# MLP up-projection as seven block products instead of the plain product

## The chip, the cores and the metric

One core of a Trainium2 chip runs the kernel. The metric is device time in microseconds (us), lower is better. The kernel before took 2957.06 us, the median of 2 runs (2955.55 to 2958.57). The engines are TensorE (PE, matrix products), VectorE (DVE), ScalarE (ACT), GpSimd (POOL) and SyncE (SP, which issues the DMA transfers).

## The reference

One layer of a bidirectional encoder over 512 tokens of width 2048: neighbourhood attention and a gated delta scan are projected, gated and mixed, and an MLP follows. Only the MLP and what stands just ahead of it matter here:

```python
    mixed = jax.nn.sigmoid(gate_a) * (y_a @ w_proj_a) + jax.nn.sigmoid(gate_b) * (y_b @ w_proj_b)
    h = h + mixed @ w_out                                    # 2048 x 2048
    hn = _rmsnorm(h, norm_mlp_w)
    h = h + jnp.square(jax.nn.relu(hn @ w_mlp_up)) @ w_mlp_down   # 2048 x 8192, 8192 x 2048
return _rmsnorm(h, norm_final_w)
```

All of it is float32.

## The kernel before

A float32 product is made from three fast products. Every operand is split into a high part (a rounded copy, made by an ACT cast) and a low part (source minus high part, made by a DVE subtract), and each 128x128 weight block takes part in three matmuls: high by high, high by low, low by high (`unit_mm`, lines 106 to 119; the matmuls are L115, L116 and L117). Weights come from HBM in units of 128x1024 (512 KB, `load_raw`, DMA on SP at L82) into one of 4 buffers; `load_unit` splits a unit by an ACT cast (L89) and a DVE subtract (L90) into one of 3 buffer pairs `wh`, `wl`. A unit serves eight 128x128 blocks, 24 matmuls with all 512 tokens as the moving tile. The activations stay in SBUF as pairs of 128x512 tiles, transposed (channels on the partitions), most of them in the pool `big` of 48 tiles.

The stages of interest follow one another:

- w_out (L850 to L864, tiles `ps_b<-mh,wh_wo`): 16 output tiles m, two units each. L855 adds x, L856 stores the sum, L861/L862 scale it by the norm weight and split it into `hh`, `hl`, and `sumsq` (L821 to L827) gathers squares. For m of 8 and more, `hh` and `hl` lie in a separate pool `hq` on the right side of SBUF, else in `big`.
- `stat` turns the sums of squares into the factor `rB` per token (matmuls L833/L834, a chain of small DVE operations L142 to L145, matmul L149, ACT copy). It runs beside the first matmuls of the next stage.
- MLP up (L866 to L879, tiles `ps_b<-hh,wh_up`): 64 output tiles m, two units each. L872 takes relu and multiplies by `rB`, L873 squares, L874 stores the 128x512 result to HBM (`hidD`). From m = 41 on, every second m one finished hidden tile is loaded back and split (`load_hid`, L841 to L844), 11 in all, so that the next stage finds them.
- MLP down (L887 to L896): four passes over 16 hidden tiles each, accumulated in `Ha`, which is first loaded from HBM (L881/L882).
- The last two output tiles of the last pass use half the tokens at a time: 128x256 matmuls, L926 to L928. The final norm ends the kernel.

A scheduler in the framework fixes the order of each engine's instructions when the kernel is built; all DMA issues of these stages share SP's one queue. An engine executes in that order and waits on semaphores. A buffer that is reused is written only after its last reader is done; a pool that is opened after another one was closed takes over its space under the same rule.

## Time and profile before

| what | value |
|---|---|
| median of the runs | 2957.06 us (2955.55 to 2958.57) |
| span of the profiled execution | 2960.0 us |
| PE busy | 98% of the span |
| DVE busy | 46% |
| ACT busy | 29% |
| DMA | 411.95 MB, mean 139 GB/s |
| w_out stage | 1360.1 to 1534.2 us |
| MLP up stage | 1534.2 to 2243.9 us |
| MLP down stage | 2243.9 to 2918.8 us, halves to 2943.2 us |

The page sums each engine's busy time over the whole span. A matmul's own duration in it overlaps those of its neighbours, so the rate of PE is read from the number of matmuls in a stretch or from the distance of their starts. Where an engine's idle time ends, the page names what was waited for last.

### The profile page before, as it was taken

The numbers are of one execution on the slowest core, as the hardware profiler recorded it, in microseconds if no ns is written. First come the engines' busy times: TensorE is split into PE (matmuls) and PEld (weight loads), VectorE is DVE, ScalarE is ACT, GpSimd is POOL, SyncE is SP. The second block draws the span as 40 slices with busy tenths as digits, with TensorE's granted clock in tenths as the row PEclk, the third lists the DMA queues.
The fourth block names the chain that finished last, engine by engine and source line by source line (L and its number), as shares of the span: only waits on it lengthen the run. The fifth ranks groups of instructions, "written<-read, shape, count | busy, mean of one in ns | idle before, by whom it ended". The sixth has DMA issues, their size and how long they took to land.

```text
span 2960.0 us, 33906 instructions
## 1 busy us (share of the span) xinstructions
PE 2913.1 (98%) x13432; PEld 2397.5 (81%) x13432; DVE 1365.7 (46%) x2071; ACT 872.6 (29%) x1333; POOL 24.7 (1%) x66
## 2 busy tenths in 40 slices
PE   8999999999999999999999999999999999999998
PEld 6778788888788888888888888888888888888887
DVE  6888769744554443444342222223333242332333
ACT  6444322233233333222222222222223131221322
POOL 0000000000000000000000000000000000000000
PEclk9999999999999999999999999999999999999999
DMA  7556653655532223443433333334336243342322
GB/s 228 185 182 186 207 185 118 219 153 171 183 114 96 91 85 132 160 155 117 148 125 114 123 119 118 120 118 136 128 129 230 94 155 100 107 143 94 113 100 86
DMA packets 170847, 411.95 MB, mean 139 GB/s; under 512 B 34368, under 2 KB 46720, under 8 KB 170688
## 3 DMA queue, kind: packets, MB, share of 16 engines
q1 hardware_dynamic: 170016, 407.69, 41.7%
q0 software_dynamic: 672, 2.10, 0.3%
q8 instruction: 105, 1.72, 0.2%
q14 instruction: 54, 0.44, 0.0%
HBM read 350.84 MB, written 58.88 MB: 138 GB/s over the span
## 4 chain that ended last, share of the span: by engine, by line
PE 72%; DVE 0%; SPq 0%; DMA 0%; ACT 0%; issue 0%; DVEq 0%; POOL 0%
PE ps_b L115 20%; PE ps_b L116 20%; PE ps_b L117 20%; PE ps_mm L117 4%; PE ps_mm L115 3%; PE ps_mm L116 3%; PE ps_ax L676 0%; PE ps_b L926 0%; PE ps_b L927 0%; PE ps_b L928 0%; DVE Ha L906 0%; PE ps_ax L137 0%; PE ps_ax L690 0%; PE ps_ax L692 0%; PE ps_ax L691 0%; PE ps_ax L657 0%
## 5 line engine op out<-in xcount | busy, mean ns | idle before, releaser
L115 PE MATMUL ps_mm<-xh,wh_in 128*128 128x512 f32 x1416 | 567.3, 401 | 3.4 <-ACT wh_in L89 3.4
L117 PE MATMUL ps_mm<-xh,wl_in 128*128 128x512 f32 x1416 | 560.6, 396 | 1.3 <-DVE wl_in L90 1.3
L116 PE MATMUL ps_mm<-xl,wh_in 128*128 128x512 f32 x1416 | 560.0, 395 | 0.0
L115 PE MATMUL ps_b<-hh,wh_up 128*128 128x512 f32 x1024 | 402.0, 393 | 0.0
L117 PE MATMUL ps_b<-hh,wl_up 128*128 128x512 f32 x1024 | 401.7, 392 | 0.0
L116 PE MATMUL ps_b<-hl,wh_up 128*128 128x512 f32 x1024 | 401.5, 392 | 0.0
L116 PE MATMUL ps_b<-hil,wh_dn 128*128 128x512 f32 x992 | 385.8, 389 | 0.0
L117 PE MATMUL ps_b<-hih,wl_dn 128*128 128x512 f32 x992 | 385.7, 389 | 0.0
L115 PE MATMUL ps_b<-hih,wh_dn 128*128 128x512 f32 x992 | 385.7, 389 | 0.0
L117 PEld LDWEIGHTS ps_mm<-xh,wl_in 128*128 128x128 f32 x1416 | 267.8, 189 | 62.3 <-DVE wl_in L90 2.6
L115 PEld LDWEIGHTS ps_mm<-xh,wh_in 128*128 128x128 f32 x1416 | 267.7, 189 | 59.1 <-ACT wh_in L89 4.0
L116 PEld LDWEIGHTS ps_mm<-xl,wh_in 128*128 128x128 f32 x1416 | 267.8, 189 | 54.7 <-issue 0.2
L89 ACT CAST wh_in<-raw_in 128x1024 fp32r<-128x1024 f32 x177 | 186.0, 1051 | 414.5 <-PE ps_mm L116 325.7
L89 ACT CAST wh_up<-raw_up 128x1024 fp32r<-128x1024 f32 x128 | 134.6, 1052 | 529.1 <-PE ps_b L116 300.0
L90 DVE TENSOR_TENSOR wl_up<-raw_up,wh_up 128x1024 fp32r<-128x1024 f32 x128 | 156.8, 1225 | 274.5 <-ACT wh_up L89 274.5
L90 DVE TENSOR_TENSOR wl_in<-raw_in,wh_in 128x1024 fp32r<-128x1024 f32 x177 | 216.2, 1222 | 121.4 <-ACT wh_in L89 114.8
L89 ACT CAST wh_dn<-raw_dn 128x1024 fp32r<-128x1024 f32 x124 | 130.9, 1055 | 477.1 <-PE ps_b L116 461.5
L90 DVE TENSOR_TENSOR wl_dn<-raw_dn,wh_dn 128x1024 fp32r<-128x1024 f32 x124 | 151.9, 1225 | 244.4 <-ACT wh_dn L89 244.1
L116 PEld LDWEIGHTS ps_b<-hl,wh_up 128*128 128x128 f32 x1024 | 192.2, 188 | 43.8 <-issue 0.2
L115 PEld LDWEIGHTS ps_b<-hh,wh_up 128*128 128x128 f32 x1024 | 192.2, 188 | 43.6 <-issue 0.2
L117 PEld LDWEIGHTS ps_b<-hh,wl_up 128*128 128x128 f32 x1024 | 192.1, 188 | 43.4
L116 PEld LDWEIGHTS ps_b<-hil,wh_dn 128*128 128x128 f32 x992 | 186.2, 188 | 38.9 <-DVE hil L95 0.2
(307 smaller groups left out, 3203.1 us busy)
## 6 DMA issues: line engine op xcount, KB each, us to landing
raw_in<-in_win SPq DMA_DIRECT2D x177, 512.0 KB
raw_up<-in_wup SPq DMA_DIRECT2D x128, 512.0 KB
raw_dn<-in_wdn SPq DMA_DIRECT2D x124, 512.0 KB
raw_wo<-in_wout SPq DMA_DIRECT2D x32, 512.0 KB
hidD<-ur SPq DMA_DIRECT2D x64, 256.0 KB
hr<-hidD SPq DMA_DIRECT2D x64, 256.0 KB
gD<-g SPq DMA_DIRECT2D x32, 256.0 KB
raw_pa<-in_wpa SPq DMA_DIRECT2D x16, 512.0 KB
```

The lines of the kernel that those rows point to most:

```text
L89: S_.copy(out=hi, in_=raw)
L90: V.tensor_tensor(out=lo, in0=raw, in1=hi.bitcast(F32), op=ALU.subtract)
L115: PE.matmul(ps, hi[:, w], rh, start=first and kk == 0, stop=False)
L116: PE.matmul(ps, hi[:, w], rl, start=False, stop=False)
L117: PE.matmul(ps, lo[:, w], rh, start=False, stop=last and kk == 7)
```

## The change

The up-projection is rewritten as a block product of the Strassen family (Winograd's form, with seven products). Rows and columns of the weight are halved: for an iteration i the four 128x1024 weight units A11, A12 (output tile m0 = i//8*16 + i%8, its two halves of the contraction) and A21, A22 (output tile m0 + 8) face the four quarters of the activations, X11, X21 (contraction halves, first 256 tokens) and X22 (second contraction half, last 256 tokens) with X12 only inside combinations. There are 32 iterations. Each makes four sums of weight units on DVE (128x1024): S1 = A21 + A22, S3 = A21 + A11, S2 = S1 + A11, S4 = S2 + A12 (signs are absorbed elsewhere), and seven products of 24 matmuls with 128x256 moving tiles: A11 by X11, S2 by T2, S1 by T1, A12 by X21, S3 by T3, S4 by X22, A22 by T4. T1 to T4 are combinations of the quarters, made once. Seven weight operands per iteration are split by ACT and DVE where the kernel before split four units for the same two output tiles. The epilogue combines the products in 128x256 pieces: two ACT copies out of PSUM and nine DVE operations, then two squares and two stores of 128x512.

What moves with it: the w_out loop visits its tiles in the order 0, 8, 1, 9 and so on; the scaling (now L868) comes after the squares; each pair of tiles makes X11 (in a new right-side pool `bq`), X21, X22 and four 128x256 combinations into a tile `TR` of a right-side pool `tr`; after the last pair 32 splits turn these into T2, T1, T3, T4. Then `tr` is closed and the pool `sm` (raw buffers for A21, the sums, small temporaries) is opened on the same space. The first iteration takes its S4 product second. The 11 early loads of hidden tiles are gone; 16 `load_hid` follow the loop.

In the order of DVE, around the start of the changed stage (XT*o*_*j* are the 128x256 low halves of T*o*; S1_0 is the sum S1 of iteration 0, `wl_` a low half of a weight operand), the change has:

```order
L95 TENSOR_TENSOR XT4_5_12137<-TR5_11742,XT4_5_12137 128x256
L95 TENSOR_TENSOR XT4_6_12140<-TR6_11894,XT4_6_12140 128x256
L95 TENSOR_TENSOR XT4_7_12143<-TR7_12045,XT4_7_12143 128x256
L926 TENSOR_TENSOR S1_0_12158<-raw_A21_0_12152,raw_A22_0_12154 128x1024
L927 TENSOR_TENSOR S3_0_12159<-raw_A21_0_12152,raw_A11_0_12150 128x1024
L934 TENSOR_TENSOR S2_0_12170<-S1_0_12158,raw_A11_0_12150 128x1024
L936 TENSOR_TENSOR S4_0_12171<-S2_0_12170,raw_A12_0_12156 128x1024
L95 TENSOR_TENSOR wl_S4_0_12231<-S4_0_12171,wh_S4_0_12230 128x1024
L95 TENSOR_TENSOR wl_A12_0_12262<-raw_A12_0_12156,wh_A12_0_12261 128x1024
```

All 32 splits of the combinations stand ahead of the first weight sum on DVE, and that sum reads raw_A21_0. On SP at the same place (raw_A11_0 is the load of A11 of iteration 0):

```order
L82 DMA raw_A11_0_12150<-in_wup 128x1024 [waits DMAHW7_49,DVE_49]
L82 DMA raw_A22_0_12154<-in_wup 128x1024 [waits DMAHW0_49,DVE_49]
L866 DMA hTD_93<-xr14_11820 128x512 [waits DMAHW1_49,DVE_49]
L82 DMA raw_A12_0_12156<-in_wup 128x1024 [waits DMAHW2_49,DVE_49]
L82 DMA raw_A11_1_12415<-in_wup 128x1024 [waits DMAHW5_49,DMAHW3_49,DVE_49]
L866 DMA hTD_93<-xr7_11900 128x512 [waits DMAHW4_49,DVE_49]
L866 DMA hTD_93<-xr15_11972 128x512 [waits DVE_49]
L893 DMA raw_A21_0_12152<-in_wup 128x1024 [waits DMAHW6_49,DVE_49]
L893 DMA raw_A21_1_12417<-in_wup 128x1024 [waits DMAHW7_49]
```

The load of A21_0 waits for a DVE instruction, the last of the 32 splits (XT4_7), whose source shares the space of its buffer; the other three units of iteration 0 are loaded ahead of it. In the middle of the stage DVE had in the kernel before, for one output tile, two low halves and one epilogue operation:

```order
L90 TENSOR_TENSOR wl_up40_0_14616<-raw_up40_0_14613,wh_up40_0_14615 128x1024
L90 TENSOR_TENSOR wl_up40_1_14646<-raw_up40_1_14643,wh_up40_1_14645 128x1024
L872 SCALAR_TENSOR_TENSOR ur39_14608<-ps_b_14547,rB_79 128x512
L90 TENSOR_TENSOR wl_up41_0_14681<-raw_up41_0_14678,wh_up41_0_14680 128x1024
L90 TENSOR_TENSOR wl_up41_1_14711<-raw_up41_1_14708,wh_up41_1_14710 128x1024
```

and now for a cycle of two output tiles (i = 4, with sums for i = 5; from the low half of A11 of i = 4 on):

```order
L95 TENSOR_TENSOR wl_A11_4_13143<-raw_A11_4_13120,wh_A11_4_13142 128x1024
L956 TENSOR_TENSOR u2_3_12902<-ps_b_12899,u2_3_12902 128x256
L957 SCALAR_TENSOR_TENSOR ur3_12903<-u2_3_12902,rB_79 128x256
L95 TENSOR_TENSOR wl_S2_4_13173<-S2_4_13140,wh_S2_4_13172 128x1024
L961 TENSOR_TENSOR t1_3_12900<-ps_b_12898,t1_3_12900 128x256
L926 TENSOR_TENSOR S1_5_13363<-raw_A21_5_13357,raw_A22_5_13359 128x1024
L962 SCALAR_TENSOR_TENSOR ur11_12904<-t1_3_12900,rB_79 128x256
L95 TENSOR_TENSOR wl_S1_4_13202<-S1_4_13128,wh_S1_4_13201 128x1024
L927 TENSOR_TENSOR S3_5_13364<-raw_A21_5_13357,raw_A11_5_13355 128x1024
L95 TENSOR_TENSOR wl_A12_4_13231<-raw_A12_4_13126,wh_A12_4_13230 128x1024
L941 TENSOR_TENSOR u2_4_13137<-ps_b_13133,t1_4_13135 128x256
L95 TENSOR_TENSOR wl_S3_4_13260<-S3_4_13129,wh_S3_4_13259 128x1024
```

Between two low halves there stands a sum or an epilogue operation of 128x256 now. The load of A22 of the following iteration reuses the buffer that the low half of A11 frees.

The diff:

```diff
--- before.py
+++ after.py
@@ -843,10 +843,20 @@
             nc.sync.dma_start(out=raw, in_=hidD[k])
             return split(raw, big(f"hih{k}"), big(f"hil{k}"))
 
-        hT = []
+        p7 = ExitStack()
+        bq = p7.enter_context(tc.tile_pool(name="bq", bufs=8, side="right", reuse_waits="tile"))
+
+        def operand(src, name):
+            t = bq.tile([128, T], F32R, tag="B2", name=name) if name.startswith("X11") else big(name)
+            return split(src, t[:, 0:256], t[:, 256:512])
+
+        lo_t, hi_t = slice(0, 256), slice(256, 512)
+        XS = {}
         with ExitStack() as p5:
-            hq = p5.enter_context(tc.tile_pool(name="hq", bufs=1, side="right", reuse_waits="tile"))
-            for m in range(16):
+            tr = p5.enter_context(tc.tile_pool(name="tr", bufs=8, side="right", reuse_waits="tile"))
+            TR = []
+            xs = []
+            for n, m in enumerate(m for j in range(8) for m in (j, j + 8)):
                 ps = bank()
                 xr = ev(f"xr{m}")
                 nc.sync.dma_start(out=xr, in_=xT[:, m, :])
@@ -854,26 +864,106 @@
                     unit_mm(ps, load_unit(wout[m, u], f"wo{m}_{u}"), mix, 8 * u, u == 0, u == 1)
                 V.tensor_tensor(out=xr, in0=ps, in1=xr, op=ALU.add)
                 nc.sync.dma_start(out=hTD[m], in_=xr)
-                if m < 8:
-                    hh, hl = big(f"hh{m}"), big(f"hl{m}")
+                sq = sumsq(xr, n, f"h{m}")
+                S_.activation(out=xr, in_=xr, func=AF.Copy, scale=nlw_s[:, m : m + 1])
+                xs.append(xr)
+                if n % 2 == 0:
+                    XS["11", m] = operand(xr[:, lo_t], f"X11_{m}")
                 else:
-                    hh, hl = hq.tile([128, T], F32R, name=f"hh{m}"), hq.tile([128, T], F32R, name=f"hl{m}")
-                S_.activation(out=hh, in_=xr, func=AF.Copy, scale=nlw_s[:, m : m + 1])
-                V.scalar_tensor_tensor(out=hl, in0=xr, scalar=nlw_s[:, m : m + 1], in1=hh.bitcast(F32), op0=ALU.mult, op1=ALU.subtract)
-                hT.append((hh, hl))
-                sq = sumsq(xr, m, f"h{m}")
+                    j = n // 2
+                    x0, x1 = xs[n - 1], xs[n]
+                    XS["21", j] = operand(x1[:, lo_t], f"X21_{j}")
+                    XS["22", j] = operand(x1[:, hi_t], f"X22_{j}")
+                    t = tr.tile([128, 4, 256], F32, tag="tr", name=f"TR{j}")
+                    V.tensor_tensor(out=t[:, 0], in0=x0[:, lo_t], in1=x0[:, hi_t], op=ALU.subtract)
+                    V.scalar_tensor_tensor(out=t[:, 1], in0=t[:, 0], scalar=-1.0, in1=x1[:, hi_t], op0=ALU.mult, op1=ALU.subtract)
+                    V.tensor_tensor(out=t[:, 2], in0=x1[:, hi_t], in1=x0[:, hi_t], op=ALU.subtract)
+                    V.scalar_tensor_tensor(out=t[:, 3], in0=t[:, 1], scalar=-1.0, in1=x1[:, lo_t], op0=ALU.mult, op1=ALU.subtract)
+                    TR.append(t)
             tasks.append(stat("h", sq))
-            hid0 = []
-            for m in range(64):
-                ps = bank()
-                for u in range(2):
-                    unit_mm(ps, load_unit(wup[m, u], f"up{m}_{u}"), hT, 8 * u, u == 0, u == 1)
-                r = ev(f"ur{m}")
-                V.scalar_tensor_tensor(out=r, in0=ps, scalar=0.0, in1=rB, op0=ALU.max, op1=ALU.mult)
-                S_.activation(out=r, in_=r, func=AF.Square)
-                nc.sync.dma_start(out=hidD[m], in_=r)
-                if m >= 40 and m % 2 == 1 and len(hid0) < 11:
-                    hid0.append(load_hid(len(hid0)))
+            for o, e in (("T2", 1), ("T1", 0), ("T3", 2), ("T4", 3)):
+                for j in range(8):
+                    XS[o, j] = operand(TR[j][:, e], f"X{o}_{j}")
+
+        with ExitStack() as p6:
+            sm = p6.enter_context(tc.tile_pool(name="sm", bufs=1, side="right", reuse_waits="tile"))
+
+            def load_a(src, name):
+                raw = sm.tile([128, 1024], F32, tag="a", name=f"raw_{name}", bufs=2)
+                nc.sync.dma_start(out=raw, in_=src)
+                return raw
+
+            def sums(name, bufs=4):
+                return sm.tile([128, 1024], F32, tag="sum", name=name, bufs=bufs)
+
+            def et(name):
+                return sm.tile([128, 256], F32, tag="et", name=name, bufs=6)
+
+            def wsplit(raw, name):
+                hi = st.tile([128, 1024], F32R, tag="wh", name=f"wh_{name}", bufs=3)
+                lo = st.tile([128, 1024], F32R, tag="wl", name=f"wl_{name}", bufs=3)
+                return split(raw, hi, lo)
+
+            def product(ps, w, o, first=False):
+                hi, lo = w
+                for j in range(8):
+                    rh, rl = XS[o, j]
+                    c = slice(j * 128, (j + 1) * 128)
+                    PE.matmul(ps, hi[:, c], rh, start=first and j == 0, stop=False, skip_group_check=True)
+                    PE.matmul(ps, hi[:, c], rl, start=False, stop=False, skip_group_check=True)
+                    PE.matmul(ps, lo[:, c], rh, start=False, stop=j == 7, skip_group_check=True)
+                    if j % NPUMP == NPUMP - 1:
+                        pump()
+
+            for i in range(32):
+                m0 = i // 8 * 16 + i % 8
+                m1 = m0 + 8
+                a11 = load_raw(wup[m0, 0], f"A11_{i}")
+                a21 = load_a(wup[m1, 0], f"A21_{i}")
+                a22 = load_raw(wup[m1, 1], f"A22_{i}")
+                a12 = load_raw(wup[m0, 1], f"A12_{i}")
+                s1, s3 = sums(f"S1_{i}"), sums(f"S3_{i}")
+                V.tensor_tensor(out=s1, in0=a21, in1=a22, op=ALU.add)
+                V.tensor_tensor(out=s3, in0=a21, in1=a11, op=ALU.add)
+                a, b, c = (bank()[:, 0:256] for _ in range(3))
+                t1, t5, u2 = et(f"t1_{i}"), et(f"t5_{i}"), et(f"u2_{i}")
+                r0, r1 = ev(f"ur{m0}"), ev(f"ur{m1}")
+                s2, s4 = sums(f"S2_{i}"), sums(f"S4_{i}")
+                product(a, wsplit(a11, f"A11_{i}"), "11", True)
+                S_.copy(out=t1, in_=a)
+                V.tensor_tensor(out=s2, in0=s1, in1=a11, op=ALU.add)
+                if i == 0:
+                    V.tensor_tensor(out=s4, in0=s2, in1=a12, op=ALU.add)
+                    product(c, wsplit(s4, f"S4_{i}"), "22", True)
+                    S_.copy(out=t5, in_=c)
+                    product(a, wsplit(a12, f"A12_{i}"), "21")
+                product(b, wsplit(s2, f"S2_{i}"), "T2", True)
+                V.tensor_tensor(out=u2, in0=b, in1=t1, op=ALU.add)
+                product(c, wsplit(s1, f"S1_{i}"), "T1", i > 0)
+                if i == 0:
+                    V.tensor_tensor(out=t5, in0=c, in1=t5, op=ALU.subtract)
+                else:
+                    S_.copy(out=t5, in_=c)
+                    product(a, wsplit(a12, f"A12_{i}"), "21")
+                V.scalar_tensor_tensor(out=r0[:, lo_t], in0=a, scalar=0.0, in1=rB[:, lo_t], op0=ALU.max, op1=ALU.mult)
+                product(b, wsplit(s3, f"S3_{i}"), "T3")
+                V.tensor_tensor(out=t5, in0=b, in1=t5, op=ALU.add)
+                V.tensor_tensor(out=t5, in0=t5, in1=t1, op=ALU.add)
+                V.scalar_tensor_tensor(out=r1[:, hi_t], in0=t5, scalar=0.0, in1=rB[:, hi_t], op0=ALU.min, op1=ALU.mult)
+                if i > 0:
+                    V.tensor_tensor(out=s4, in0=s2, in1=a12, op=ALU.add)
+                    product(c, wsplit(s4, f"S4_{i}"), "22")
+                V.tensor_tensor(out=u2, in0=c, in1=u2, op=ALU.add)
+                V.scalar_tensor_tensor(out=r0[:, hi_t], in0=u2, scalar=0.0, in1=rB[:, hi_t], op0=ALU.max, op1=ALU.mult)
+                S_.activation(out=r0, in_=r0, func=AF.Square)
+                nc.sync.dma_start(out=hidD[m0], in_=r0)
+                product(b, wsplit(a22, f"A22_{i}"), "T4")
+                V.tensor_tensor(out=t1, in0=b, in1=t1, op=ALU.add)
+                V.scalar_tensor_tensor(out=r1[:, lo_t], in0=t1, scalar=0.0, in1=rB[:, lo_t], op0=ALU.min, op1=ALU.mult)
+                S_.activation(out=r1, in_=r1, func=AF.Square)
+                nc.sync.dma_start(out=hidD[m1], in_=r1)
+            hid0 = [load_hid(k) for k in range(16)]
+        p7.close()
 
         hp = p1.enter_context(tc.tile_pool(name="hp", bufs=1, side="right", reuse_waits="tile"))
         Ha = hp.tile([128, 16, T], F32, name="Ha")
```

## Rows read from the trace of the kernel before

**Rows 1.** windows of the up and the down stage; (x) is the count

```profile
core 0: us, PE busy (x) PEld busy (x) DVE busy (x) ACT busy (x) POOL busy (x), PEclk, DMA share, GB/s
...
1900.00:2100.00 200.00, 200.00 (x871) 163.09 (x870) 59.68 (x59) 50.07 (x59) 0.00 (x0) 1.00 0.38 127
2600.00:2800.00 200.00, 200.00 (x884) 165.60 (x883) 65.87 (x70) 47.82 (x53) 0.00 (x0) 1.00 0.33 110
```

**Rows 2.** waits of PE, 1180 to 2960 us: us in total, times, longest us

```profile
PE ps_b L149 <- DVE dg_f L145: 2.9, 1, 2.9
```

**Rows 3.** timeline of PE in the up stage, every 24th matmul; start, duration

```profile
1907.86 0.39 PE L115 MATMUL ps_b<-hh,wh_up 128*128 128x512 f32 x1
...
1913.45 0.39 PE L115 MATMUL ps_b<-hh,wh_up 128*128 128x512 f32 x1
...
1918.90 0.39 PE L115 MATMUL ps_b<-hh,wh_up 128*128 128x512 f32 x1
```

**Rows 4.** timeline of PE at the 128x256 halves; start, duration

```profile
2919.01 0.28 PE L926 MATMUL ps_b<-hih,wlh 128*128 128x256 f32 x1
2919.13 0.28 PE L927 MATMUL ps_b<-hil,wlh 128*128 128x256 f32 x1
...
2924.77 0.28 PE L926 MATMUL ps_b<-hih,wlh 128*128 128x256 f32 x1
```

**Rows 5.** groups of the 128x256 halves, 2919 to 2945 us; columns in the first line

```profile
line engine op names shapes xcount | busy us, mean ns | idle before us <-releasers
...
L931 DVE TENSOR_TENSOR Ha<-ps_b,Ha 128x256 f32<-128x256 f32 x4 | 1.7, 420 | 8.1 <-PE ps_b L928 8.1
```

**Rows 6.** groups of the up stage, 1700 to 2240 us

```profile
L90 DVE TENSOR_TENSOR wl_up<-raw_up,wh_up 128x1024 fp32r<-128x1024 f32 x96 | 117.6, 1225 | 203.8 <-ACT wh_up L89 203.8
L89 ACT CAST wh_up<-raw_up 128x1024 fp32r<-128x1024 f32 x96 | 101.0, 1052 | 395.3 <-PE ps_b L116 224.9 <-issue 170.4
```

**Rows 7.** instructions of L590, a 128x256 ACT copy: ns min/median/max

```profile
L590 ACT COPY vn<-ps_ax x32: 365/373/381, 611.2 to 841.2; 128x256 f32<-128x256 f32 x32
```

**Rows 8.** timeline of DVE and ACT at the start of the up stage

```profile
1534.66 0.69 DVE L855 TENSOR_TENSOR xr<-ps_b,xr 128x512 f32<-128x512 f32 x1 [3.31 <-PE ps_b L117]
1535.56 1.23 DVE L90 TENSOR_TENSOR wl_up<-raw_up,wh_up 128x1024 fp32r<-128x1024 f32 x1 [0.21 <-ACT wh_up L89]
1536.70 0.75 DVE L862 SCALAR_TENSOR_TENSOR hl<-xr,nlw_s,hh 128x512 fp32r<-128x512 f32 x1
1539.06 0.16 DVE L142 TENSOR_SCALAR rsa_h<-ps_s 128x4 f32<-128x4 f32 x1 [1.62 <-PE ps_s L834]
...
1541.44 0.69 DVE L145 TENSOR_TENSOR dg_h<-ident,rsy_h 128x512 f32<-128x512 f32 x1
...
1536.05 0.62 ACT L822 ACTIVATE sqh<-xr 128x512 f32<-128x512 f32 x1
```

**Rows 9.** timeline of SP in the up stage, and windows beside it

```profile
1909.51 0.33 SPq L82 DMA_DIRECT2D raw_up<-in_wup  x1
...
1910.50:1911.50 1.00, 1.00 (x6) 0.82 (x5) 0.00 (x0) 0.00 (x0) 0.00 (x0) 1.00 0.85 197
1911.50:1912.50 1.00, 1.00 (x6) 0.80 (x5) 0.00 (x0) 0.00 (x0) 0.00 (x0) 1.00 0.80 328
1912.50:1913.50 1.00, 1.00 (x6) 0.80 (x5) 0.55 (x1) 0.73 (x1) 0.00 (x0) 1.00 0.00 0
```

**Rows 10.** timeline of PE, and a window, behind an early gap

```profile
36.14 0.50 PE L115 MATMUL ps_mm<-xh,wh_in 128*128 128x512 f32 x1 [3.42 <-ACT wh_in L89]
...
38.00 0.63 PE L115 MATMUL ps_mm<-xh,wh_in 128*128 128x512 f32 x1
...
38.00:40.00 2.00, 2.00 (x6) 1.62 (x5) 0.00 (x0) 1.47 (x3) 0.00 (x0) 0.50 0.62 190
```

**Rows 11.** timeline of SP and ACT behind the up stage

```profile
2255.21 2.34 SPq L843 DMA_DIRECT2D hr<-hidD  x4
...
2260.63 1.95 ACT L94 CAST hih<-hr 128x512 fp32r<-128x512 f32 x3 [2.52 <-DMA hr<-hidD]
```

## The prediction

> **What bounds the kernel now.** I read the waits of PE first. Over the stages from 1180 us to the end the largest total is a single wait of 2.9 us [rows 2], and it lies in the final norm. So TensorE has work all the time, and the time of a stage is its number of matmuls times their distance. The windows by stage say the same and add the rate: 871 matmuls of 128x512 in 200 us in the up stage, 884 in the down stage, with the granted clock at 1.00 and DVE busy 59.68 of 200 us [rows 1]. That is 0.2296 and 0.2262 us per matmul. DVE, ACT and the DMA have room; they matter only where the change takes that room.
>
> The timeline of PE shows why the up stage is the slower one. From one unit's first matmul to the next unit's, 24 matmuls, it takes 5.59 us in one half of an output tile and 5.45 us in the other [rows 3]: 0.233 and 0.227 us each. The slow half is the one whose activations lie in the right-side pool `hq`. I take the place of the tile for the cause, without proof, since only X11 lies in such a pool in the change.
>
> **The products.** The change replaces 64 x 2 x 24 = 3072 matmuls of 512 columns by 32 x 7 x 24 = 5376 of 256 columns. That is 7/8 of the columns. Seven eighths of the time is not what it costs, because a matmul of half the columns takes more than half the distance. The halves of the last two tiles show this: starts at 2919.01 and 2919.13, and 48 matmuls later, with every step alike, 2924.77 [rows 4]. So 5.76 / 48 = 0.120 us, against 0.1133 for half of 0.2267. The moving tile there is a 256-column half of a 512-column tile, three matmuls per weight block, a new block each time: the same form as the new products. Six products out of seven are charged 0.120. For X11 I add half of the 0.006 us that separate the two halves of a tile, so 0.123. After: 4608 x 0.120 + 768 x 0.123 = 647.4 us. Before: 3072 x 0.2300 = 706.6 us (the mean of 0.233 and 0.227). **Gain 59.2 us.** The ends of this price: half of a 512-column matmul, 0.1133, would give 609 us; and 0.1267, as far above 0.120 again as that lies above the half, would give 681 us. I take 0.120, since it is the same operation.
>
> The Trainium skill ("TensorE: Matmul & The Clock Gate", section Back-to-back issue gap) puts the gap of a single matmul at N/2.4 + 2.5 ns, which is 109 ns for 256 columns. By it the new products would come to 587 us, an estimate from that page. Row and page differ by 11 ns at 256 columns [rows 4]; the rows are this kernel's, and they decide.
>
> **The start of the stage.** This is the main new cost. The first weight sum reads A21_0. Its load waits for the last of 32 splits of the combinations, since its buffer lies on the space of the TR tiles; and these splits stand behind the last w_out tile and the norm's chain on DVE. PE has one product that needs none of this, A11 by X11. It enters the stage at 1534.2, has 24 x 0.123 = 3.0 us of it, and the eight narrow matmuls of `stat`. These need the squares of the last tile, which now come ahead of the scaling: after 1534.66 + 0.69 and 0.62 us on ACT, at about 1536.0 [rows 8]. In the kernel before the matmuls took 2.4 us from the end of the squares (1536.67) to L142 (1539.06) [rows 8]; so L142 starts at 1538.4 now and PE is idle from 1539.2. DVE's chain from L142 to the end of L145 is 3.07 us [rows 8]: 1541.5. Then five 128x256 operations for the last pair, then the 32 splits. A 128x256 operation is 0.42 us [rows 5], but the next one starts up to 0.09 us before its end (1535.56 + 1.23 against 1536.70) [rows 8], so 0.33 to 0.42 apart; at 0.38 the 37 take 14.1 us: 1555.6. ACT runs ahead with its casts at 0.37 us [rows 7]. The load: issued at 1909.51, its bytes move until 1912.5 and none after [rows 9], so 3.2 us with some margin: 1558.8. Four sums on 128x1024, priced as the subtract of that shape, 1.225 us [rows 6] and 1.14 apart: 1563.5. ACT's cast of S4, 1.05 us [rows 6]: **PE goes on at 1564.5, after an idle stretch of 25.3 us.** The ends, from 0.33 and 0.42 us per small operation and 3.0 to 5.4 us for the load, are 23 and 29 us.
>
> After two matmuls PE needs the low half of S4, 1.2 us on DVE: 1.0 us. After a gap of 3.42 us at 32.7 us, the granted clock was 0.50 (1.2 GHz) a little later [rows 10]. I charge one stretch at half clock, as long as that gap, 3.4 us: 1.7 us lost. From there on iteration 0 has its four operands, and A21_1 is already there.
>
> **The steady state.** PE needs 24 x (6 x 0.120 + 0.123) = 20.2 us per iteration. DVE does seven low halves and four sums, 11 x 1.225 = 13.5 us, and nine 128x256 operations, 9 x 0.42 = 3.8 us [rows 5, 6]: 17.3 us, 86%. ACT does seven casts of 1.05 us, two copies of 0.37 and two squares of 0.62: 9.4 us [rows 6 to 8]. Per iteration 4 x 0.524 + 2 x 0.262 = 2.62 MB are moved, 130 GB/s, as now (127) [rows 1]. So PE stays the bound, and DVE's and ACT's work is free as long as no load holds DVE up. The tightest loop is that of A22: its load is issued when the low half of A11 has freed the buffer; the sum S1 waits for it; and from S1 to the next low half of A11, DVE has ten operations of 1.225 and six of 0.42 us, 14.8 us. With 3.2 us for the load that is 18.0 of 20.2 us. The loop fits as long as a load lands within 5.4 us. Behind a late load stand, on DVE, the epilogue of the iteration before and the next low halves, for which PE waits.
>
> The w_out stage gets 128x256 splits and combinations instead of one 128x512 split per tile: seven per pair of tiles, 2.9 us, in place of two operations of 0.75 us [rows 5, 8]. Of the 21.8 us that PE needs for a pair, DVE is then busy less than 11. I cost it at nothing. PE would be held only if the casts of the next units came late; these are made two units, 10.9 us, ahead.
>
> **The end of the stage.** Eleven hidden tiles were ready for the down stage; now two are, at the last product's end. Two more wait for the last square on ACT, the others for four buffers behind the last store. PE works two output tiles at once, so four hidden tiles last 4 x 6 x 0.2267 = 5.4 us. The first reload behind the store is issued about 2 us after the end; in the kernel before, amid the loads of `Ha`, a reload issued from 2255.21 on was cast at 2260.63, 5.4 us [rows 11]. With cast and subtract it is ready at about 8.7 us: PE waits 3.3 us, and little more for the rest. Ends: 1 us (a load of 3.2 us) and 8 us (three groups of four, each late). I take 4.
>
> **Sum.** -59.2 + 25.3 + 1.0 + 1.7 + 4.0 = -27.2 us. The profiled execution spans 2960.0 us and becomes 2933; the median of the runs, 2957.06, becomes **2930 us**. What a measurement can tell from no change is about 2%, 59 us: 2898 and 3016.
>
> **The rivals.**
>
> *The first load does not wait, or the splits go faster.* Then the stall is a few us and the time about 2905. Against it speaks the order of SP and DVE, which leaves no other way for the first sum. 0.06.
>
> *256-column matmuls are dearer in a long stretch.* The rows cover 192 of them with DVE mostly idle; now 5376 run beside a DVE at 86%. At 0.1267 the time is 2964, at 1.5% over 0.120 (as up over down stage) 2937. 0.14.
>
> *The loop of DVE and loads becomes the bound, and the kernel is slower.* Place: the wait of S1 for A22. A load that lands in L us makes the iteration 14.8 + L. It costs from L = 5.4 on; the gain is used up at 0.85 us per iteration (27.2 / 32), L = 6.3; and 3016 is reached at 2.7 us, L = 8.1. At L = 7 the time is 2930 + 32 x 1.6 = 2981. For it: a landing of 5.4 us has been seen [rows 11], and SP issues in order, so a store that waits holds the loads behind it. Against it: that was amid 16 other loads, while the up stage moves the same bytes per us as before. 0.12, of which 0.05 beyond 3016.
>
> *The fixed part of a matmul vanishes.* At 0.1133 us throughout, 38.3 us less than in the sum: about 2892. This is the way in which the rule quoted above would show. The halves [rows 4] speak against it, row by row. 0.02.
>
> The forecast has 0.66, with its own ends (stall 23 to 29, end 1 to 8, 0.119 to 0.1215 us per matmul) at about 2918 to 2945.
>
> **How the numbers follow.** The range reaches up over the dearer matmuls and the mild loop, and down over most of the absent stall: 2907 to 2966; outside lie the vanished fixed part, part of the absent stall, and the loop from L = 6.5 on, under 0.2 together. Faster by over 2%: 0.02 and part of the absent stall, 0.04. Slower by over 2%: 0.05. Within: 0.91.
>
> **What would show it.** The forecast is right if the starts in the new stage lie 0.120 us apart at a granted clock of 1.00, if PE has one gap of about 25 us near 1540 that ends with ACT's cast of S4, and if there are no waits of PE in the 31 later iterations (20.2 us each). A wait of S1 for the load of A22 in each iteration would show the loop; matmuls 0.122 us apart or more, the second rival. It is wrong altogether if PE waits once per iteration for something not listed here, such as an accumulator bank that an epilogue operation frees late.

## The result and the profile after

The changed kernel took 2926.62 us, the median of 2 runs (2922.42 to 2930.82), beside 2957.06: a ratio of 0.9896, 95% interval 0.9859 to 0.9932. Four more runs narrowed that (run `again` below): 0.9898, 0.9883 to 0.9912, which is 30 us less, within 26 to 35. The forecast was 2930 us.

The profiled execution spans 2920.6 us, 39.4 less than that of before. Not all of it belongs to the change. The table divides both spans by the starts of the first and the last high-by-high matmul of the up stage and of the first one of the 128x256 halves.

| stretch | before | after | difference |
|---|---|---|---|
| start to the first matmul of the up stage | 1534.5 | 1526.9 | -7.6 |
| first to last matmul of the up stage | 709.0 | 672.2 | -36.8 |
| from there to the 128x256 halves (down stage) | 675.5 | 680.5 | +5.0 |
| halves and final norm | 41.0 | 41.0 | 0 |

Of the first line the change touches only the w_out stage, and that takes 173.4 us before and 173.5 after (first to last start of its L115). The 7.6 us are there when w_out begins, at 1360.4 and at 1352.8 us; `again` shows what they are. The other lines give -31.8 us. The bounds are in these rows, the first of before and the others of after ([rows 4] has the first of the halves before): instructions of one kind, then ns min/median/max and the first and last start in us.

```profile
L115 PE MATMUL ps_b<-hh,wh_up x1024: 389/392/791, 1534.5 to 2243.5; 128*128 128x512 f32 x171
...
L912 PE MATMUL ps_b<-X,wh_A x512: 278/283/366, 1526.9 to 2190.4; 128*128 128x256 f32 x171
...
L912 PE MATMUL ps_b<-XT,wh_A x256: 279/283/384, 1573.1 to 2199.1; 128*128 128x256 f32 x128
...
L1016 PE MATMUL ps_b<-hih,wlh x64: 277/283/467, 2879.6 to 2903.5; 128*128 128x256 f32 x64
```

The windows of the up stage after (columns in the first line), which answer to [rows 1]:

```profile
core 0: us, PE busy (x) PEld busy (x) DVE busy (x) ACT busy (x) POOL busy (x), PEclk, DMA share, GB/s
...
1530.00:1555.30 25.30, 1.74 (x14) 1.54 (x14) 19.78 (x54) 12.69 (x38) 0.00 (x0) 0.60 0.21 70
...
1555.30:1562.00 6.70, 6.65 (x35) 5.62 (x36) 5.77 (x5) 3.48 (x5) 0.00 (x0) 0.72 0.39 133
...
1584.00:1784.00 200.00, 200.00 (x1672) 200.00 (x1671) 167.12 (x200) 91.37 (x110) 0.00 (x0) 1.00 0.40 131
```

In the middle of the stage there are 1672 matmuls in 200 us, 0.1196 us each, PE is always busy at a granted clock of 1.00 (2.4 GHz), and DVE is busy 167 of 200 us instead of 60. At the start there are 25 us in which PE does next to nothing, and behind them 6.7 us in which the granted clock is 0.72, the mean of stretches at 1.2 and at 2.4 GHz. PE's waits from the up stage to the halves, which answer to [rows 2] (total, times, longest in us), and the wait of its weight loads (PEld) for the low half of S4:

```profile
PE ps_b L912 <- ACT wh_S L94: 23.6, 1, 23.6
...
PE ps_b L117 <- DVE wl_dn L90: 1.3, 2, 0.7
...
PE ps_b L115 <- ACT hih L94: 1.0, 3, 0.4
...
PEld ps_b L914 <- DVE wl_S L95: 0.5, 1, 0.5
```

One wait of 23.6 us at the start, and small ones in the down stage, for the reloaded hidden tiles and for low halves of its weights; none in the 31 later iterations. The timelines of DVE, SP, ACT and PE around the long wait, where [rows 8] stood before (start, duration, and in brackets the idle time ahead and what ended it):

```profile
1535.03 10.81 DVE L95 TENSOR_TENSOR XT<-TR,XT 128x256 fp32r<-128x256 f32 x32
...
1549.47 1.22 DVE L926 TENSOR_TENSOR S<-raw_A,raw_A 128x1024 f32<-128x1024 f32 x1 [3.62 <-DMA raw_A<-in_wup]
...
1553.00 1.22 DVE L936 TENSOR_TENSOR S<-S,raw_A 128x1024 f32<-128x1024 f32 x1
...
1545.87 0.33 SPq L893 DMA_DIRECT2D raw_A<-in_wup  x1
...
1554.26 1.04 ACT L94 CAST wh_S<-S 128x1024 fp32r<-128x1024 f32 x1 [9.63 <-DVE S L936]
...
1555.35 0.58 PE L912 MATMUL ps_b<-X,wh_S 128*128 128x256 f32 x1 [23.61 <-ACT wh_S L94]
```

They show the chain in its order: 32 splits from 1535.03 on; 0.03 us after them SP issues the load of A21_0; DVE waits 3.62 us for it; four sums; ACT's cast of S4; PE. The product of X11, which lies in the right-side pool, runs from 1817.02 to 1819.87, behind one on a tile of `big`:

```profile
1814.14 0.28 PE L912 MATMUL ps_b<-XT,wh_A 128*128 128x256 f32 x1
...
1817.02 0.28 PE L912 MATMUL ps_b<-X,wh_A 128*128 128x256 f32 x1
...
1819.87 0.28 PE L912 MATMUL ps_b<-XT,wh_S 128*128 128x256 f32 x1
```

2.85 and 2.88 us for 24 matmuls: the place in the right-side pool costs nothing here.

### The profile page after: what moved, and what is told of

Read it like the earlier page. It is cut to its first block, busy times and chain, and to the rows that moved or that the text cites. A ratio compares the mean times of both kernels' runs of the same rounds, so it can differ in the third digit from the quotient of the medians.

```text
span 2920.6 us, 39434 instructions
## 1 busy us (share of the span) xinstructions
PE 2850.9 (98%) x15736; PEld 2462.6 (84%) x15736; DVE 1723.6 (59%) x2592; ACT 1017.2 (35%) x1549; POOL 24.8 (1%) x66
## 4 chain that ended last, share of the span: by engine, by line
PE 87%; DMA 6%; DVE 5%; issue 1%; ACT 1%; SPq 0%; DVEq 0%; ACTq 0%
PE ps_b L117 11%; PE ps_b L115 11%; PE ps_b L116 11%; PE ps_mm L115 9%; PE ps_mm L117 9%; PE ps_mm L116 9%; PE ps_b L912 7%; PE ps_b L913 7%; PE ps_b L914 7%; DMA bB<-rowD 1%; DMA Nd<-bB 1%; DVE wl_in L90 1%; DMA kb<-rowD 0%; DMA XQ<-Nd 0%; PE ps_ax L589 0%
## 5 line engine op out<-in xcount | busy, mean ns | idle before, releaser
L115 PE MATMUL ps_mm<-xh,wh_in 128*128 128x512 f32 x1416 | 565.9, 400 | 3.2 <-ACT wh_in L89 3.2
L115 PE MATMUL ps_b<-hih,wh_dn 128*128 128x512 f32 x992 | 386.6, 390 | 1.0 <-ACT hih L94 1.0
L115 PEld LDWEIGHTS ps_mm<-xh,wh_in 128*128 128x128 f32 x1416 | 267.1, 189 | 58.4 <-ACT wh_in L89 3.6
L115 PEld LDWEIGHTS ps_b<-hih,wh_dn 128*128 128x128 f32 x992 | 186.2, 188 | 42.0 <-ACT hih L94 3.4
L117 PEld LDWEIGHTS ps_b<-hih,wl_dn 128*128 128x128 f32 x992 | 186.2, 188 | 40.1 <-DVE wl_dn L90 2.1
L914 PE MATMUL ps_b<-XT,wl_S 128*128 128x256 f32 x768 | 217.3, 283 | 0.0
L913 PE MATMUL ps_b<-XT,wh_S 128*128 128x256 f32 x768 | 217.3, 283 | 0.0
L912 PE MATMUL ps_b<-XT,wh_S 128*128 128x256 f32 x768 | 217.2, 283 | 0.0
L94 ACT CAST wh_S<-S 128x1024 fp32r<-128x1024 f32 x128 | 134.1, 1048 | 211.7 <-PE ps_b L913 202.1
L95 DVE TENSOR_TENSOR wl_S<-S,wh_S 128x1024 fp32r<-128x1024 f32 x128 | 156.6, 1223 | 31.5 <-ACT wh_S L94 29.0
L983 DVE TENSOR_TENSOR Ha<-ps_b,Ha 128x512 f32<-128x512 f32 x62 | 42.9, 692 | 189.2 <-PE ps_b L117 189.2
```

What stands on the lines that cost most here:

```text
L94: S_.copy(out=hi, in_=src)
L95: V.tensor_tensor(out=lo, in0=src, in1=hi.bitcast(F32), op=ALU.subtract)
L115: PE.matmul(ps, hi[:, w], rh, start=first and kk == 0, stop=False)
L117: PE.matmul(ps, lo[:, w], rh, start=False, stop=last and kk == 7)
L912: PE.matmul(ps, hi[:, c], rh, start=first and j == 0, stop=False, skip_group_check=True)
L913: PE.matmul(ps, hi[:, c], rl, start=False, stop=False, skip_group_check=True)
```

## The experiments

### again: the changed kernel once more

Nothing is changed in it.

> The changed kernel once more, in five rounds. By the stages of its profile the up stage is 37.3 us shorter (672.5 against 709.7) and the down stage 5.4 us longer (679.5 against 674.1); 7.3 us of the 39.4 us between the two profiled spans lie ahead of the first changed instruction. Theory: those 7.3 us are a matter of the single execution, and the true gain is 32 us, 2925 us beside 2957. Rival: the change moves the earlier stages too, and the gain is 39 us, 2918 us.

Measured: 2928.11 us beside 2957.90 us, ratio 0.9898 (0.9883 to 0.9912). In its profile the first matmul of the up stage starts at 1533.4 us, 1.1 us from where it started before, and the up stage lasts 671.9 us. So the early 7.6 us came with that one execution, and the change is worth 30 us. All traces of this case reach w_out between 1352.3 and 1364.2 us, ahead of any edit; so single runs below are compared by their stages and not by their total times.

### narrow256: narrow tiles without the block products

```diff
-                for u in range(2):
-                    unit_mm(ps, load_unit(wup[m, u], f"up{m}_{u}"), hT, 8 * u, u == 0, u == 1)
+                units = [load_unit(wup[m, u], f"up{m}_{u}") for u in range(2)]
+                for ts in (slice(0, 256), slice(256, 512)):
+                    for u in range(2):
+                        unit_mm(ps[:, ts], units[u], hT, 8 * u, u == 0, u == 1, lambda t: t[:, ts])
```

> The kernel before, with the plain up-projection, but each unit used on two 256-column halves of the tokens: 6144 matmuls of 128x256 in place of 3072 of 128x512; loads, splits and epilogue stay. Theory (a matmul costs its columns and a fixed part of some 13 ns, whatever stands around it): 6144 x 0.1196 = 735 us against 706.6, 28 us longer, about 2985 us; both halves of an output tile at 0.1196 us, since X11 in its right-side pool ran at that too. Rival (the fixed part comes from the new stage's busier DVE, and half the columns cost half the time elsewhere): no change, 2957 us.

Measured: 2982.7 us, ratio 1.0081 (1.0064 to 1.0098), 25 us more. A window of the up stage, the group of its first matmuls, and the first matmul of a unit on `big` tiles, of the next on `hq` tiles, and of the one behind it:

```profile
1600.00:1800.00 200.00, 200.00 (x1679) 200.00 (x1678) 56.23 (x54) 47.29 (x54) 0.00 (x0) 1.00 0.34 115
...
L115 PE MATMUL ps_b<-hh,wh_up x2048: 277/283/679, 1531.9 to 2267.1; 128*128 128x256 f32 x187
...
1809.36 0.28 PE L115 MATMUL ps_b<-hh,wh_up 128*128 128x256 f32 x1
...
1812.23 0.28 PE L115 MATMUL ps_b<-hh,wh_up 128*128 128x256 f32 x1
...
1815.08 0.28 PE L115 MATMUL ps_b<-hh,wh_up 128*128 128x256 f32 x1
```

The stage lasts 735.2 us, 26.2 more than before. At 0.1191 us per matmul, with DVE busy only 56 of 200 us, the fixed part is there without the new stage's DVE work. The 24 matmuls take 2.87 us on `big` tiles and 2.85 us on `hq` tiles. The same columns in twice as many matmuls cost 26 us; the block products save an eighth of them. What the fixed part consists of is not shown: the weight loads (PEld) are busy for all 200 us here and for 163 us of 200 at 512 columns [rows 1], so it could lie with them.

### swaphq: the slow half of the plain product

```diff
-                if m < 8:
+                if m >= 8:
                     hh, hl = big(f"hh{m}"), big(f"hl{m}")
```

> The kernel before, with the first eight activation tiles in the pool hq and the last eight in big, the other way round than it was. Theory of the prediction (a moving tile of 512 columns that lies in hq costs 0.233 us, one in big 0.227): the slow half of each output tile is now the first unit, not the second; the time is the same, since as many lie in hq. Rival (the second unit of an output tile is slow wherever its activations lie): the second unit stays at 0.233 us.

Measured: 2961.63 us in one run, the up stage 709.0 us as before. The last matmul of one output tile, then of the next tile's first unit, on `hq` tiles, and of its second, on `big` tiles:

```profile
1900.18 0.39 PE L117 MATMUL ps_b<-hh,wl_up 128*128 128x512 f32 x1
...
1905.77 0.39 PE L117 MATMUL ps_b<-hh,wl_up 128*128 128x512 f32 x1
...
1911.22 0.39 PE L117 MATMUL ps_b<-hh,wl_up 128*128 128x512 f32 x1
```

5.59 us for the first unit, 5.45 for the second: it was the other way round in [rows 3]. The slowness goes with the pool, for 512 columns. At 256 columns it is absent, for `hq` (narrow256) and, in the other pool, for X11 above. Why, no run here shows.

### start1: an early load of A21_0, and A12 second

```diff
+        ap = p7.enter_context(tc.tile_pool(name="ap", bufs=1, side="right", reuse_waits="tile"))
...
+                if name == "A21_0":
+                    raw = ap.tile([128, 1024], F32, name=f"raw_{name}")
+                else:
+                    raw = sm.tile([128, 1024], F32, tag="a", name=f"raw_{name}", bufs=2)
...
+                    product(a, wsplit(a12, f"A12_{i}"), "21")
                     product(c, wsplit(s4, f"S4_{i}"), "22", True)
                     S_.copy(out=t5, in_=c)
-                    product(a, wsplit(a12, f"A12_{i}"), "21")
```

> The changed kernel with two edits at the start of the stage: A21 of iteration 0 has a buffer of its own and is loaded early, and the product A12 by X21 of iteration 0 comes ahead of S4 by X22. Theory (the gap of 23.6 us is a chain on DVE, in which the load is only the last 3.6 us): DVE's wait of 3.6 us goes, PE has 2.9 us more work, and its idle time at the start falls to 17 us. Rival (the late load is the gap): the sums come as soon as the load is there, and the idle time falls to 5 us or less.

Measured: 2917.41 us in one run; the up stage lasts 665.1 us, 7.1 less than after. PE's waits at the start, the matmul at which S4 begins, ACT around the copy that PE waited for, and DVE's 32 splits with the first sum:

```profile
PE ps_b L916 <- ACT t L937: 10.7, 1, 10.7
...
PE ps_b L916 <- ACT wh_S L94: 2.1, 2, 1.7
...
PE ps_b L149 <- DVE dg_h L145: 1.8, 1, 1.8
...
1536.18 7.76 ACT L94 CAST XT<-TR 128x256 fp32r<-128x256 f32 x25 [0.24 <-DVE TR L880]
...
1547.24 0.37 ACT L937 COPY t<-ps_b 128x256 f32<-128x256 f32 x1 [2.83 <-DVE XT L95]
...
1554.14 0.39 PE L916 MATMUL ps_b<-X,wh_S 128*128 128x256 f32 x1 [1.67 <-ACT wh_S L94]
...
1537.40 10.82 DVE L95 TENSOR_TENSOR XT<-TR,XT 128x256 fp32r<-128x256 f32 x32
...
1548.25 1.23 DVE L930 TENSOR_TENSOR S<-raw_A,raw_A 128x1024 f32<-128x1024 f32 x1
```

14.6 us of waits instead of 23.6, where 17 were expected for the theory and 5 or less for the rival. The load was not the gap: the first sum no longer waits for it, but still stands behind 32 splits on DVE. The first wait has a new name, though: the product A12 by X21 adds to the accumulator that ACT has to copy first. That copy stood behind 25 casts on ACT (1536.18 on), and what ended its last 2.83 us of waiting was a split on DVE: its target `t` lies in the pool `sm`, on the space of the TR tiles that the splits read.

### best2: half of the splits behind the sums

```diff
-            for o, e in (("T2", 1), ("T1", 0), ("T3", 2), ("T4", 3)):
-                for j in range(8):
-                    XS[o, j] = operand(TR[j][:, e], f"X{o}_{j}")
+            splits("T2", "T1")
+            iteration(0, load_a0, lambda name: tr.tile([128, 1024], F32, tag="ta", name=name),
+                      lambda name: next(ets), splits)
...
+            splits("T3")
             product(b, wsplit(s3, f"S3_{i}"), "T3")
...
-                if i == 0:
+                if i in (0, 31):
```

The edits of start1 are in it too. The combinations lie in two sets of tiles; the sums of iteration 0 reuse the set of T2 and T1. The target of ACT's copy in iteration 0 lies in a buffer `sq` of the norm's squares, no longer on the space of the combinations.

> start1 with the first 16 splits of the combinations (T2, T1) ahead of the weight sums of iteration 0 and the other 16 (T3, T4) behind them, and with the last iteration in the order of the first. Theory (the gap is DVE's chain): 16 splits at 0.34 us less ahead of the first sum, so 5.4 us less idle time of PE at the start than in start1 (14.6 us), about 9 us, and an up stage of about 660 us (start1 665). Rival (the norm's chain or the ACT casts set the gap): under 2 us less than start1.

Measured: 2911.76 us in one run; the up stage lasts 661.4 us, 3.7 less than start1. PE's longest wait with the matmul that ends it, ACT's copy, and DVE's 16 splits with the first sum behind them:

```profile
PE ps_b L865 <- ACT wh_S L94: 10.4, 2, 10.3
...
1545.90 0.58 PE L865 MATMUL ps_b<-X,wh_S 128*128 128x256 f32 x1 [10.28 <-ACT wh_S L94]
...
1531.20 0.37 ACT L886 COPY sq_et<-ps_b 128x256 f32<-128x256 f32 x1 [3.29 <-PE ps_b L867]
...
1534.45 5.45 DVE L95 TENSOR_TENSOR XT<-TA,XT 128x256 fp32r<-128x256 f32 x16
...
1539.82 1.22 DVE L879 TENSOR_TENSOR S<-raw_A,raw_A 128x1024 f32<-128x1024 f32 x1
```

The first sum follows the 16th split without a pause. The product of S4 begins 19.5 us after the first matmul of the stage, at 1526.4, and in start1 24.8 us after it, at 1529.3: DVE's chain is 5.3 us shorter, as the theory said. PE's waits at the start, with the small ones, fell less, to 11.2 us, 3.4 below start1: the copy out of the accumulator now comes early, so that A12 by X21 runs ahead of the gap, at a granted clock of 1.00, and not inside it at 0.60. The stage gained 3.7 us; of what was lost behind S4, 0.6 us is a new wait in the last iteration, and the rest is not shown.

### best3: hidden tiles reloaded in the last iteration

```diff
+            def early():
+                for k in range(0, 8, 2):
+                    raw = sm.tile([128, 1024], F32, tag="a", name=f"raw_h{k}", bufs=2)
+                    for e in range(2):
+                        h = raw[:, e * T : (e + 1) * T]
+                        nc.sync.dma_start(out=h, in_=hidD[k + e])
+                        hid0.append(split(h, big(f"hih{k + e}"), big(f"hil{k + e}")))
...
+            early()
             product(c, wsplit(s1, f"S1_{i}"), "T1", i not in (0, 31))
```

> best2 with eight hidden tiles reloaded during the last iteration, through the two buffers of A21 that are idle by then, onto the operands X21 and X22 that the last iteration's order frees early. Theory (the down stage is longer because its first tiles come late): the down stage loses under 2 us instead of 5 to 6, and with the shorter start the kernel takes about 2912 us, 16 us less than the changed kernel. Rival (the reloads collide with the loads of Ha, early or late): 3 us or more are still lost, about 2916 us.

Measured: 2912.21 us (5 runs), ratio to before 0.9854 (0.9840 to 0.9867). From the last matmul of the up stage to the halves it takes 676.9 us: 1.4 more than before, where the changed kernel lost 5.0, `again` 6.1, and best2, the same but for the reloads, 5.3 (680.8 us).

```profile
PE ps_b L115 <- ACT hih L94: 1.2, 2, 1.0
```

So the late tiles were the cost. This is the version to keep: 43 us better than the kernel before by the ratio, where the changed kernel is 30 us better; the medians of the two, 2912.21 and 2928.11 us, are 16 us apart.

### best4: the norm's statistics later

```diff
-            tasks.append(stat("h", sq))
...
+            mid()      # tasks.append(stat("h", sq)), in iteration 0
             product(b, wsplit(s2, f"S2_{i}"), "T2", True)
```

The buffers `sq` are three instead of two.

> best3 with the norm's statistics put behind the product S4 by X22 of iteration 0, so that their chain on DVE (3.07 us) no longer stands ahead of the splits and sums. Theory (DVE's chain up to S4 sets the gap): the idle time of PE at the start falls by 3 us from 11.2 us, the time to about 2909 us. Rival (another engine's part, the store of the last w_out tile and the ACT scaling that waits for it, ends last): under 1 us.

Measured: 2913.88 us (5 runs), ratio to before 0.9846 (0.9833 to 0.9859), no different from best3.

```profile
1534.37 0.16 DVE L142 TENSOR_SCALAR rsa_h<-ps_s 128x4 f32<-128x4 f32 x1 [3.86 <-PE ps_s L834]
...
PE ps_b L865 <- ACT wh_S L94: 11.5, 2, 11.3
```

The gap did not shrink. The scheduler put only the later half of the chain behind the splits. Its first operations still stood ahead of them and now waited 3.86 us for PE's later matmuls. The edit did not do what it was made for, so it does not tell the two expectations apart. Its trace gives an estimate: ACT's scaling, which the first operation behind that half of the chain reads, had ended at 1533.75, and that operation started at 1535.44; so moving the whole chain could still give about 1.7 us.

### nopre: the kernel before without the early reloads

```diff
-            hid0 = []
...
-                if m >= 40 and m % 2 == 1 and len(hid0) < 11:
-                    hid0.append(load_hid(len(hid0)))
+            hid0 = [load_hid(k) for k in range(16)]
```

> The kernel before, with the 11 early reloads of hidden tiles taken out and all 16 behind the loop, as in the change; nothing else. Theory (the longer down stage comes from the reloads alone): PE loses 4 to 6 us in the first 30 us of the down stage, as it does in the changed kernel (5.4). Rival (it comes from the shape of the last iteration, with its epilogue and stores): PE loses under 1.5 us.

Measured: 2975.66 us in one run. The up stage is the same (709.0 us); from its last matmul to the halves it takes 685.8 us, 10.3 more than before. PE's wait and two windows:

```profile
PE ps_b L115 <- ACT hih L94: 5.2, 3, 4.1
...
2244.00:2254.00 10.00, 5.69 (x21) 3.67 (x19) 3.28 (x4) 2.19 (x3) 0.00 (x0) 0.93 0.60 189
...
2254.00:2264.00 10.00, 9.14 (x31) 7.21 (x31) 5.70 (x9) 5.76 (x10) 0.00 (x0) 0.73 0.85 274
```

Late reloads cost that much with the plain product's last iteration too, so its new shape is not needed for the loss; the size was under-estimated. Behind the wait of 4.1 us, which ends at 2252.19, the granted clock is 0.73 over the window from 2254 on, a mean of stretches at 1.2 and 2.4 GHz; that comes on top of the wait. In the changed kernel two tiles were there at the end, the waits stay under a microsecond each, and the granted clock stays at 1.00: 5 to 6 us.

### dve2 and dve4: more work for DVE

```diff
+            dum = sm.tile([128, 1024], F32, name="dum")
...
                 V.tensor_tensor(out=s3, in0=a21, in1=a11, op=ALU.add)
+                for _ in range(2):    # dve4: range(4)
+                    V.tensor_tensor(out=dum, in0=s1, in1=s3, op=ALU.add)
```

> The changed kernel with two more 128x1024 additions on DVE in each iteration, whose result nobody reads. Theory (PE is the bound, DVE has 3.3 us of room per iteration of 20.1 us): 16.8 + 2 x 1.14 = 19.1 us of DVE, no change in the 31 later iterations, 2 us at the start. If the loop of sum, split and load of A22 is as tight as 14.8 + 3.2 us, it comes to 20.3 us now and costs up to 6 us in all. Rival (DVE's order already holds PE, and 0.1196 us per matmul is its pace): 2.3 us per iteration, 73 us more.

> The same with four more additions per iteration: 16.8 + 4 x 1.14 = 21.4 us of DVE against 20.1 us of PE. Theory: DVE is the bound, 1.3 us per iteration, 40 us more over the stage, and somewhat more if the loads, which wait for DVE, come late too (up to 60). Rival (room on DVE is larger than its busy share says): under 10 us more.

Measured, one run each: dve2 2928.29 us with an up stage of 674.8 us, 2.6 more than after, about 1.2 of it at the start; dve4 2937.62 us with 685.6 us, 13.4 more. A window of the stage in dve2, a late one with a late sum S1, and the first window in dve4:

```profile
1700.00:1900.00 200.00, 200.00 (x1672) 200.00 (x1671) 185.31 (x220) 90.90 (x110) 0.00 (x0) 1.00 0.40 130
...
1975.00:2175.00 200.00, 199.50 (x1657) 198.62 (x1656) 178.18 (x217) 87.94 (x109) 0.00 (x0) 1.00 0.38 127
...
2126.17 1.23 DVE L928 TENSOR_TENSOR S<-raw_A,raw_A 128x1024 f32<-128x1024 f32 x1 [2.07 <-DMA raw_A<-in_wup]
```

```profile
1700.00:1900.00 200.00, 199.05 (x1642) 196.97 (x1642) 197.73 (x233) 89.41 (x108) 0.00 (x0) 1.00 0.40 130
```

Up to about 1975 us dve2 leaves the rate of PE as it was, 1672 matmuls in 200 us. From 1983 us on S1 waits for its load in each of the last ten iterations, 1.5 to 2.6 us, and PE falls to 1657 in 200 us. That is the sign that the prediction named for the loop of DVE and loads (the view does not tell A21 from A22). It put that loop at 18.0 of 20.2 us, and two additions, 2.3 us, about use up its room; why only the last iterations show it is open. In dve4 no sum behind the start waits for a load; there are 1642 matmuls in the window, and 168, one iteration, take 20.5 us instead of 20.1. Here DVE itself is the bound, as the theory said, but it costs 13 us and not 40, between theory and rival: four additions, 4.5 us, are slightly more than fits. My figure of 40 us came from busy time. Operations of DVE overlap at their ends; in dve4, where DVE is busy for 197.7 of 200 us, they start 1.13 us apart though each lasts 1.22:

```profile
1806.32 1.22 DVE L95 TENSOR_TENSOR wl_S<-S,wh_S 128x1024 fp32r<-128x1024 f32 x1
...
1807.45 1.22 DVE L958 TENSOR_TENSOR S<-S,raw_A 128x1024 f32<-128x1024 f32 x1
...
1808.59 1.22 DVE L95 TENSOR_TENSOR wl_A<-raw_A,wh_A 128x1024 fp32r<-128x1024 f32 x1
```

With 1.13 and 0.33 us an iteration needs 11 x 1.13 + 9 x 0.33 = 15.4 us of DVE in the changed kernel, and 19.9 in dve4; short pauses between some operations make up the 20.5 us that were measured.

## Why the prediction was right, point by point

- **The products.** 59.2 us expected; 5376 x 0.1196 = 643.0 us against 706.6 is 63.6. The price of 0.120, from the rows of the 128x256 halves [rows 4], held over 5376 matmuls and beside a busy DVE. narrow256 shows it without the block products. The surcharge for X11 was wrong, though its reason was sound at 512 columns (swaphq); it is 2.3 us of the 4.4 by which this term was too small. The rows of [rows 3] begin three matmuls behind a unit's first; from first to first (1907.16, 1912.75, 1918.21 us) it is 5.59 and 5.46 us, so the reading holds.
- **The start.** 25.3 us expected, 23.6 measured, with the chain that was told: splits, load, sums, cast. Of the 1.7 us most lies in the splits: they ran 0.34 us apart (10.81 us for 32, not 12.2). The norm's chain began some 0.6 us earlier beside the end of PE's work than told, and the load took 3.6 us, not 3.2.
- **Low half and clock.** After the gap the granted clock was 0.72 over 6.7 us, which loses up to 1.9 us; 1.7 were charged. The wait for the low half was 0.5 us; 1.0 was charged.
- **The steady state.** Costed at nothing beside PE: no wait of PE in 31 iterations. The loop through the load of A22 did not bind, and its room was near the 20.2 - 18.0 us of the prediction: the two additions of dve2, 2.3 us, bring the waits for a load in the last ten iterations. DVE's room by itself was larger than its busy time says (dve4). The w_out stage, costed at nothing too, took 173.5 us beside 173.4.
- **The end.** 4 us expected, 5.0 and 6.1 measured; best3 gives back all but 1.4, so it was the late tiles.
- **Sum.** -63.6 + 23.6 + 0.5 (the wait for the low half) + 1.9 + 5.0 = -32.6 us by terms, -31.8 by the stages, -30 by the runs; -27.2 was forecast. The errors of the products (-4.4), the start (-1.7), the low half (-0.5), the clock (+0.2) and the end (+1.0) leave 5.4 us. That 2930 lies within 2 us of the 2928.11 of `again` is partly luck: the scatter between executions is larger than that.
- **The rivals.** Dearer matmuls: no, 0.1196 us (the 2937 us that this rival gives at 1.5% over 0.120 are 2938 to 2940 by its own numbers). A DVE loop that binds: not in this kernel; with two more additions per iteration it begins to. A vanished fixed part: no. By the Trainium skill ("TensorE: Matmul & The Clock Gate", section Back-to-back issue gap) the gap of a single matmul would have been 109 ns at 256 columns; the trace has 119 to 120 ns at both loads of DVE, and the measurement decides.
- **The first rival**, a start without the wait, did not come: the splits ran faster than costed, but that is 1.7 us of the gap. It shrinks when their order is changed (start1, best2).

## What to carry to other kernels

A product count that falls to 7/8 is not a time that falls to 7/8: price the new tile shape by a stretch of the trace with that same shape before counting the gain. Then look at the two ends of the stage. Here 64 us were gained in the middle, and 31 of them were paid back where operands had to be made before the first product and where the next stage had lost its early loads; an early load, another order of splits and products and eight early reloads brought 13 to 16 us back. When asking whether an engine off the critical path has room, count the distance of its starts, not its busy time, and look for the first operation that begins to wait for a load.

## What the runs showed of the hardware that was not expected

- A matmul's distance at the granted clock of 1.00 was 0.1191 to 0.1200 us at 256 columns and 0.2262 to 0.2271 at 512 on tiles of `big`: 0.107 us for 256 columns more, which leaves some 0.013 us that do not shrink between these two widths.
- At 0.50 (1.2 GHz) nothing is left over: 14 steps from 1548.05 to 1551.03 us in start1 are 0.213 us each, twice 0.107, and at 512 columns, behind the early gap of [rows 10], a step was 0.426 us. So the fixed part cannot be added to every matmul.

```profile
1548.05:1551.03 2.98, 2.98 (x15) 2.98 (x15) 2.95 (x4) 0.00 (x0) 0.00 (x0) 0.50 0.86 333
```

- Nor does the line of the two widths go on to narrow tiles: the norm's float32 matmuls with one moving column leave two records each, and in the changed kernel these start 0.11 us apart too, at 1.00. What sets that distance, no run here shows.

```profile
1529.08 0.36 PE L834 MATMUL ps_s<-ones,sqh 128*128 128x1 f32 x2
1529.30 0.36 PE L833 MATMUL ps_s<-ones,sacc 128*128 128x1 f32 x2
```

- Moving tiles of 512 columns in the pool `hq` cost 0.233 us instead of 0.227, wherever in the output tile they come (swaphq); at 256 columns the same pool costs nothing (narrow256).
- DVE's back-to-back operations on 128x1024 start 1.13 us apart at a duration of 1.22, those on 128x256 0.34 apart at 0.42. Where one reads what the one ahead wrote it is more: 1.25 us from S2 to S4 (1551.75 to 1553.00) and 0.45 from L956 to L957 (1570.11 to 1570.56) after.
